# An encoder with expert-choice routing: ranking tokens in four groups of tiles, the last norm without delay, softmax two turns after the logits

## The chip, the cores and the metric

The kernel runs on 1 core of one Trainium2 chip. The metric is the device time of one execution in microseconds (us); of several runs the median is given. Engines are called PE (TensorE, matmuls), DVE (VectorE), ACT (ScalarE), POOL (GpSimd) and SP (the queue that issues most loads).

## What is computed

Two layers. Each has a mixer sub-layer (four branches, gates, an output projection) and an expert-choice mixture of experts; after each comes a layer norm. The change concerns the place where one goes over into the other:

```python
x = layer_norm(DEEPNORM_ALPHA * x + mix, ln1_g[l], ln1_b[l])        # mix: output projection of the mixer
cap = EC_FACTOR * T // N_EXPERTS                                    # 128 of 1024 tokens
aff = softmax(einsum('btd,de->bte', x, w_router))                   # 16 experts
gate, idx = lax.top_k(swapaxes(aff, 1, 2), cap)                     # each expert takes its 128 best tokens
xs = x[idx]                                                         # gather, then SwiGLU of each expert
```

The kernel doesn't sort indices. It finds for each expert the 128th largest affinity (the threshold), and then compares all affinities with it.

## The kernel before

1024 tokens are 8 tiles of 128 rows. In the output projection (`out_main`) PE works through the tiles in order, 48 matmuls of 512 columns each (L325 to L327, into the banks `pz`; three matmuls stand for one product in higher precision). As soon as half a tile is summed, DVE adds the residual and takes statistics (L1269, L1270).

What follows on a tile is the generator `post`: it ends the statistics (L420, L421 on DVE, L422 on POOL), turns the tile over (L1240 on PE, L1242 on ACT), forms the router logits on PE (`logits`, L1287), the softmax (`affinities`, L1294 to L1299: DVE, with the exponential L1297 on ACT), and the norm itself (`ln_apply`). In the norm, `spread` says how many of the two halves go over ACT (L432) and POOL (L433, L434); the others are two DVE instructions (L436, L437). Then the normed tile is stored twice, to X1 (L1234), from which the experts gather, and to XA (L1235), to which they add. These DMAs are issued by POOL; the X1 store of the last tile is issued by ACT.

After tiles 3, 5 and 7 a generator `topk_stage` starts, which ranks the affinities of a group of tiles (0 to 3, 4 and 5, 6 and 7). It turns the affinities over (L1343 on PE, a copy by ACT to `tkb`: L1346, or L1350 behind a DVE memset L1348 where there are fewer than 32 rows), takes the 64 largest of each half row by 8 rounds of MAX and MATCH_REPLACE on DVE (L1354, L1357), brings the halves together (L1330 moves rows to other partitions with a small matmul on PE, L1360 reads them), and sorts them by 7 pairs of DVE instructions (`ordered`: L1321 takes maxima, L1322 minima). Rows of several tiles are then merged two by two (L1330, `join` L1334, `ordered`), and merged with the best 128 so far, `TK`. The last group ends in the threshold (L1370). `topk` then counts and places the chosen tokens, and the first expert gathers (L1448) and begins on PE.

The order on every engine is the order in which the generators yield. At each turn of the main loop `side_all` gives every waiting `post` one step and every waiting `topk_stage` three steps. During the projection a stage puts in six idle steps (`lag`) at some places.

```python
        for _ in range(3):
            for g in list(lows):
```

Weights of the experts are loaded by SP into 45 shared slots meanwhile; ACT and DVE split them into two parts (L129, L130). The third sort buffer `tkb` is one of these slots too.

Of the kernel before, what the change touches and what calls it, by code (L numbers as in the profile page):

```python
# [22 lines left out]
NE = 16  # L23
# [129 lines left out]
def tile_encoder_trunk(ctx: ExitStack, tc: tile.TileContext, I, out, dbg=None, depth=DEPTH):  # L153
# [13 lines left out]
    def half(shape, dtype=F32, name="h"):  # L167
        return hp_.tile(shape, dtype, tag="H", name=name)
# [119 lines left out]
    sides, posts, lows = [], [], []  # L288
# [11 lines left out]
    def side_all():  # L300

        for g in list(posts):
            try:
                next(g)
            except StopIteration:
                posts.remove(g)
        for _ in range(3):
            for g in list(lows):
                try:
                    next(g)  # L310
                except StopIteration:
                    lows.remove(g)
        return [side_step(), bool(posts or lows)]
# [111 lines left out]
    def ln_apply(zs, mv, g, b, o, spread=1):  # L425

        if spread:
            nc.vector.scalar_tensor_tensor(mv[:, 2:3], mv[:, 0:1], -1.0, mv[:, 3:4], op0=OP.mult, op1=OP.mult)
        for hf in range(2):
            ns = slice(512 * hf, 512 * hf + 512)  # L430
            if spread and hf >= 2 - spread:
                nc.scalar.activation(o[:, ns], zs[hf], AF.Identity, scale=mv[:, 3:4], bias=mv[:, 2:3])  # L432
                nc.gpsimd.tensor_tensor(o[:, ns], o[:, ns], g[:, ns], op=OP.mult)  # L433
                nc.gpsimd.tensor_tensor(o[:, ns], o[:, ns], b[:, ns], op=OP.add)  # L434
            else:
                nc.vector.scalar_tensor_tensor(o[:, ns], zs[hf], mv[:, 0:1], g[:, ns], op0=OP.subtract, op1=OP.mult)  # L436
                nc.vector.scalar_tensor_tensor(o[:, ns], o[:, ns], mv[:, 3:4], b[:, ns], op0=OP.mult, op1=OP.add)  # L437

    def halves(x):
        return [x[:, 0:512], x[:, 512:1024]]  # L440
# [748 lines left out]
    def out_main(l, L, MG, xsrc, R, nxt):  # L1189

        CV, gw = L["CV"], L.pop("wr")
        bw = half([128, 8, NE], F32, name="bw")
        gs = sm.tile([128, 2, NE], F32, name="gs", bufs=1)
        gc = sm.tile([128, 2, NE], F32, name="gc", bufs=1)
        for i, w in ((1, bw), (0, gw)):
            nc.vector.tensor_tensor(w, gw, CV[:, 60 + 8 * i:68 + 8 * i][:, :, None].to_broadcast([128, 8, NE]),
                                    op=OP.mult)
            nc.vector.tensor_reduce(gs[:, i], w.rearrange("p k e -> p e k"), axis=AX.X, op=OP.add)
        del bw, w
        L.update(gw=gw, gc=gc)  # L1200

        LG = pair([128, D], "lg")
        bcast_row(LG[0], I["ln1_g"], l * D, D, nc.sync)
        bcast_row(LG[1], I["ln1_b"], l * D, D, nc.sync)
        xz = {}

        def xload(t):
            if t < 8:
                xz[t] = slot([128, D], F32, "xr")
                nc.sync.dma_start(xz[t], xsrc[128 * t:128 * t + 128, :])  # L1210

        def post(t, x, xt, st):
            ts = slice(128 * t, 128 * t + 128)
            mv = ln_mv(st, 4.0 * EPS)
            if t == 0:
                p = bank("pl")
                nc.tensor.matmul(p[:, 0:2 * NE], ones, gs.rearrange("p a e -> p (a e)"), start=True, stop=True)
                nc.vector.tensor_copy(gc, p[:, 0:2 * NE].rearrange("p (a e) -> p a e", a=2))
            if t < 7:
                yield  # L1220
            if t == 0:
                turned(x, xt, 0)
                yield
            pl = bank("pl")
            logits(L, xt, pl, 0)
            turned(x, xt, 1)
            if t < 7:
                yield
            logits(L, xt, pl, 1)
            affinities(L, t, pl, mv, R)  # L1230
            for _ in range(6 if t == 7 else 0):
                yield
            ln_apply(halves(x), mv, LG[0], LG[1], x, spread=1 + (t > 5))
            (nc.scalar if t == 7 else nc.gpsimd).dma_start(X1[l][ts, :], x)  # L1234
            nc.gpsimd.dma_start(XA[l][ts, :], x)  # L1235

        def turned(x, xt, hf):
            p = bank("pq")
            for k in range(4):
                nc.tensor.transpose(p[:, 128 * k:128 * k + 128],  # L1240
                                    x[:, 512 * hf + 128 * k:512 * hf + 128 * k + 128], ident)
            nc.scalar.copy(xt[:, 4 * hf:4 * hf + 4], p.rearrange("p (k s) -> p k s", k=4))  # L1242

        xload(0)
        xload(1)
        wo = {}
        BUDGET = {2: 26, 3: 28, 5: 31, 6: 35}
        for t in range(8):
            mh, ml = nxt
            if t + 1 < 8:  # L1250
                nxt = out_split(MG, t + 1)
            xload(t + 2)
            x = xz.pop(t)
            st = sm.tile([128, 2, 6], F32, name="st")
            xt = slot([128, 8, 128], F32, "xt")
            pz = [bank("pz"), bank("pz")]
            cut = {0: 8, 7: 4}.get(t, 0)
            turns = [(k, nf) for k in range(cut) for nf in range(2)] + \
                    [(k, nf) for nf in range(2) for k in range(cut, 8)]
            for i, (k, nf) in enumerate(turns):  # L1260
                ns = slice(512 * nf, 512 * nf + 512)
                if t == 0 and nf == 0:
                    wo[k] = W.get(names[l, "wo", k])
                mm3(pz[nf], mh[:, k], ml[:, k], wo[k][0][:, ns], wo[k][1][:, ns], k == 0, k == 7)
                if t == 7 and nf == 1:
                    W.done(names[l, "wo", k])
                    del wo[k]
                if k == 7:
                    nc.vector.scalar_tensor_tensor(x[:, ns], x[:, ns], 2.0 * ALPHA, pz[nf], op0=OP.mult, op1=OP.add)  # L1269
                    nc.vector.bn_stats(st[:, nf, :], x[:, ns])  # L1270
                if t and (k, nf) == (6, 1):
                    turned(x, xt, 0)
                if i % 2:
                    yield
            if t in BUDGET:
                W.budget = BUDGET[t]
            if t == 6:
                W.prep_max = 0
            if t == 7:
                del nxt  # L1280
            del mh, ml
            posts.append(post(t, x, xt, st))
            del x, xt

    def logits(L, xt, p, hf):
        for k in range(4 * hf, 4 * hf + 4):
            nc.tensor.matmul(p[:, 0:NE], xt[:, k, :], L["gw"][:, k, :], start=(k == 0), stop=(k == 7))  # L1287

    def affinities(L, t, p, mv, R):

        AF_, gc = R[0], L["gc"]
        rs = sm.tile([128, 4 + NE], F32, name="rs")
        ng = rs[:, 4:4 + NE]
        nc.vector.scalar_tensor_tensor(ng, gc[:, 0], mv[:, 0:1], p[:, 0:NE], op0=OP.mult, op1=OP.subtract)  # L1294
        nc.vector.scalar_tensor_tensor(ng, ng, mv[:, 3:4], gc[:, 1], op0=OP.mult, op1=OP.subtract)
        nc.vector.tensor_reduce(rs[:, 0:1], ng, axis=AX.X, op=OP.min)
        nc.scalar.activation(AF_[:, t, :], ng, AF.Exp, scale=-1.0, bias=rs[:, 0:1], accum_out=rs[:, 1:2])  # L1297
        nc.vector.reciprocal(rs[:, 2:3], rs[:, 1:2])
        nc.vector.tensor_scalar(AF_[:, t, :], AF_[:, t, :], rs[:, 2:3], None, op0=OP.mult)  # L1299
        if t in (3, 5, 7):  # L1300
            lows.append(topk_stage(R, {3: 0, 5: 4, 7: 6}[t], t))

    def topk_stage(R, t0, t):

# [4 lines left out]
        r = NE * nt  # L1309
# [17 lines left out]
        def moved(src, lo, n):  # L1327
            p = bank("pl")
            w = src.shape[1]
            nc.tensor.matmul(p[:n, 0:w], ident[:lo + n, lo:lo + n], src[:lo + n], start=True, stop=True)  # L1330
            return p[:n, 0:w]

        def join(i, u, v, n):
            nc.vector.tensor_tensor(TB[i][:n], u[:n], v[:n, ::-1], op=OP.max)  # L1334
# [4 lines left out]
        TB = [tb[:, i, :] for i in range(8)]  # L1339
# [23 lines left out]
        if t == 7:  # L1363
            while stages[0] != t0:
                yield
            join(3, TK, TB[2], NE)
            q = moved(TB[2][:r], NE, NE)
            yield from ordered(3, NE)
            join(3, TB[4], q, NE)
            nc.vector.tensor_reduce(TK[:, 0:1], TB[3][:NE], axis=AX.X, op=OP.min)  # L1370
            return
        n, i = r, 2
# [326 lines left out]
    for l in range(depth):  # L1699
# [19 lines left out]
        R = (AF_, half([NE, 128], F32, "TK"), [0])  # L1719
# [47 lines left out]
```

## Time and profile before

| | before |
|---|---|
| median of 3 runs | 3200.58 us (3200.43 to 3203.56) |
| the profiled execution | 3198.24 us |
| its span | 3196.5 us |
| granted PE clock, mean of the span | 0.981 |
| PE, DVE, ACT, POOL busy | 3046.6, 2043.6, 1430.0, 477.5 us |

The profile is of one execution. A row of a timeline has the start, the duration, engine and line, what is written from what, shapes and the number of instructions; a bracket behind it is the time that the engine stood idle before it, and what ended that. A matmul of 512 columns is shown with 0.40 us, but the next one starts 0.23 us later: they overlap. The projection and the ranking lie at 845 to 990 us (first layer) and 2424 to 2566 us (second layer).

### The profile page before, as it was taken

What the parts mean: (1) busy time and instruction counts of PE and PEld (TensorE: products, weight loads), DVE (VectorE), ACT (ScalarE), POOL (GpSimd) and SP (SyncE); (2) the same over time, 40 slices, a digit from 0 to 9 for tenths busy, and PEclk for the clock granted to TensorE, in tenths of its full rate; (3) what the DMA queues carried; (4) which work ended last, traced back from release to release, by engine and by line L of the source; (5) the groups of instructions that cost most, each with busy time, mean ns of one, the idle gap of its engine ahead of it and who ended that gap; (6) DMA issues with size and microseconds to landing.
All of it is one profiled execution on the core that took longest, in us unless ns stands there. A gap on an engine that the chain in (4) does not pass through costs nothing. (4 is left out here: it accounts for less than half of the span.)

```text
span 3196.5 us, 42301 instructions
## 1 busy us (share of the span) xinstructions
PE 3046.6 (95%) x15438; PEld 2449.4 (77%) x15438; DVE 2043.6 (64%) x3480; ACT 1430.0 (45%) x2101; POOL 477.5 (15%) x476
## 2 busy tenths in 40 slices
PE   8999999999896999999999999999999789999997
PEld 7977887778775777777789787877787567777775
DVE  3435552227768888888872365422286788888887
ACT  3122223332225777777631222233322267777773
POOL 0000001004441100001130000100064300011003
PEclk9999999999997999999999999999999899999999
DMA  5312324227556999999622123432385679999993
GB/s 163 102 33 67 112 93 135 67 92 272 222 206 250 367 368 377 377 372 368 200 96 86 40 86 93 126 102 67 108 293 207 244 269 378 373 370 369 373 343 125
DMA packets 283089, 670.45 MB, mean 210 GB/s; under 512 B 26866, under 2 KB 125258, under 8 KB 282880
## 3 DMA queue, kind: packets, MB, share of 16 engines
q1 hardware_dynamic: 259616, 586.16, 49.7%
q0 software_dynamic: 22976, 80.54, 8.4%
q8 instruction: 121, 1.98, 0.2%
q10 hardware_dynamic: 288, 1.05, 0.1%
q14 instruction: 88, 0.72, 0.1%
HBM read 578.60 MB, written 89.06 MB: 209 GB/s over the span
## 5 line engine op out<-in xcount | busy, mean ns | idle before, releaser
L130 DVE TENSOR_TENSOR wlo<-wraw,whi 128x1024 fp32r<-128x1024 f32 x886 | 1080.1, 1245 | 525.5 <-ACT whi L129 519.7
L129 ACT CAST whi<-wraw 128x1024 fp32r<-128x1024 f32 x890 | 913.5, 1047 | 361.3 <-PE h L326 79.7
L325 PE MATMUL pb<-xh,whi 128*128 128x512 f32 x1344 | 549.1, 409 | 0.0
L326 PE MATMUL pb<-xl,whi 128*128 128x512 f32 x1344 | 528.8, 393 | 0.0
L327 PE MATMUL pb<-xh,wlo 128*128 128x512 f32 x1344 | 528.7, 393 | 0.0
L325 PE MATMUL h<-whi,xsT 128*128 128x512 f32 x960 | 397.9, 414 | 0.5 <-ACT xsT L1467 0.5
L326 PE MATMUL h<-wlo,xsT 128*128 128x512 f32 x960 | 380.1, 396 | 1.0 <-DVE wlo L130 1.0
L327 PE MATMUL h<-whi,xsT 128*128 128x512 f32 x960 | 379.5, 395 | 0.3 <-DVE xsT L1470 0.3
L325 PEld LDWEIGHTS pb<-xh,whi 128*128 128x128 f32 x1344 | 252.5, 188 | 78.5 <-issue 21.8
L327 PEld LDWEIGHTS pb<-xh,wlo 128*128 128x128 f32 x1344 | 252.3, 188 | 59.1
L326 PEld LDWEIGHTS pb<-xl,whi 128*128 128x128 f32 x1344 | 252.9, 188 | 52.5 <-issue 1.9
L1138 ACT ACTIVATE gt<-pb,CVh 128x512 f32<-128x512 f32 x128 | 87.7, 685 | 362.6 <-PE pb L327 341.1
L326 PEld LDWEIGHTS h<-wlo,xsT 128*128 128x128 f32 x960 | 181.6, 189 | 49.8 <-DVE hT L1470 7.2
L325 PEld LDWEIGHTS h<-whi,xsT 128*128 128x128 f32 x960 | 181.5, 189 | 46.9 <-issue 7.7
L327 PEld LDWEIGHTS h<-whi,xsT 128*128 128x128 f32 x960 | 181.0, 189 | 43.9 <-DVE xsT L1470 2.0
L325 PE MATMUL py<-whi,hT 128*128 128x512 f32 x512 | 205.3, 401 | 0.0
L326 PE MATMUL py<-wlo,hT 128*128 128x512 f32 x512 | 202.2, 395 | 3.0 <-DVE wlo L130 3.0
L327 PE MATMUL py<-whi,hT 128*128 128x512 f32 x512 | 202.3, 395 | 0.0
L325 PE MATMUL pa<-whi,xh 128*128 128x256 f32 (+1 forms) x640 | 187.3, 293 | 6.4 <-ACT whi L129 5.6
L326 PE MATMUL pa<-wlo,xh 128*128 128x256 f32 (+1 forms) x640 | 184.8, 289 | 2.3 <-DVE wlo L130 2.2
L327 PE MATMUL pa<-whi,xl 128*128 128x256 f32 (+1 forms) x640 | 183.8, 287 | 0.0
L1448 POOL DMA_INDIRECT xs<-X,idx x32 | 54.6, 1706 | 864.6 <-ACT whi L129 814.0
(384 smaller groups left out, 4445.1 us busy)
## 6 DMA issues: line engine op xcount, KB each, us to landing
wraw<-in_w_e_dram SPq DMA_DIRECT2D x768, 512.0 KB
wraw<-in_w_in_dram SPq DMA_DIRECT2D x100, 512.0 KB
GD<-gt SPq DMA_DIRECT2D x64, 512.0 KB
gl<-GD SPq DMA_DIRECT2D x64, 512.0 KB
Rb<-RD POOLq DMA_DIRECT2D x32, 256.0 KB, 4.8
wraw<-in_w_branch_dram SPq DMA_DIRECT2D x16, 512.0 KB
wraw<-YT SPq DMA_DIRECT2D x16, 512.0 KB
wraw<-in_w_out_dram SPq DMA_DIRECT2D x16, 512.0 KB
```

Of the source, the lines that this page charges most:

```text
L129: self.nc.scalar.copy(hi, raw)
L130: (self.nc.gpsimd if i in self.pool else self.nc.vector).tensor_tensor(lo, raw, hi.bitcast(F32), op=OP.subtract)
L325: nc.tensor.matmul(p, sh, mh, start=first, stop=False)
L326: nc.tensor.matmul(p, sh, ml, start=False, stop=False)
L327: nc.tensor.matmul(p, sl, mh, start=False, stop=last)
L1138: nc.scalar.activation(gt[:, 512 * hf:512 * hf + 512], p, AF.Tanh, scale=0.5, bias=CVh[:, j:j + 1])
L1448: nc.gpsimd.indirect_dma_start(out=xs, out_offset=None, in_=X1[l], in_offset=bass.IndirectOffsetOnAxis(ap=idx[:, :1], axis=0))
```

## The change

Four edits. Each turn gives the ranking four steps in place of three. The softmax of tiles 0 to 6 comes two turns after the second half of the logits. The norm of the last tile follows its softmax at once, where six turns lay between, and tile 6 uses the form with one half on DVE. The groups are now tiles 0 to 3, 4 and 5, 6, and 7; the last group is a single tile, so that its own merge falls away.

```diff
-        for _ in range(3):
+        for _ in range(4):
             for g in list(lows):
...
             logits(L, xt, pl, 1)
+            for _ in range(2 if t < 7 else 0):
+                yield
             affinities(L, t, pl, mv, R)
-            for _ in range(6 if t == 7 else 0):
-                yield
-            ln_apply(halves(x), mv, LG[0], LG[1], x, spread=1 + (t > 5))
+            ln_apply(halves(x), mv, LG[0], LG[1], x, spread=1 + (t > 6))
             (nc.scalar if t == 7 else nc.gpsimd).dma_start(X1[l][ts, :], x)
...
-        if t in (3, 5, 7):
-            lows.append(topk_stage(R, {3: 0, 5: 4, 7: 6}[t], t))
+        if t in (3, 5, 6, 7):
+            lows.append(topk_stage(R, {3: 0, 5: 4, 6: 6, 7: 7}[t], t))
...
             join(3, TK, TB[2], NE)
-            q = moved(TB[2][:r], NE, NE)
-            yield from ordered(3, NE)
-            join(3, TB[4], q, NE)
             nc.vector.tensor_reduce(TK[:, 0:1], TB[3][:NE], axis=AX.X, op=OP.min)
```

What it moves, at three places. On DVE, in the sort of the 64 rows of tiles 0 to 3 (`tkb`; `rs`, `mv` and `aff` belong to the softmax of tile 4, `xr` is its norm). Before:

```order
L1321 TENSOR_TENSOR tkb<-tkb 64x4x16
L1322 TENSOR_TENSOR tkb<-tkb 64x4x16
L1321 TENSOR_TENSOR tkb<-tkb 64x8x8
L1322 TENSOR_TENSOR tkb<-tkb 64x8x8
L1321 TENSOR_TENSOR tkb<-tkb 64x16x4
```

and now:

```order
L1322 TENSOR_TENSOR tkb<-tkb 64x4x16
L1294 SCALAR_TENSOR_TENSOR rs<-gc,mv,pl 128x16
L1295 SCALAR_TENSOR_TENSOR rs<-rs,mv,gc 128x16
L1296 TENSOR_REDUCE rs<-rs 128x1
L1298 RECIPROCAL rs<-rs 128x1
L1299 TENSOR_SCALAR aff<-aff,rs 128x16
L428 SCALAR_TENSOR_TENSOR mv<-mv 128x1
L436 SCALAR_TENSOR_TENSOR xr<-xr,mv,lg_6438 128x512
L437 SCALAR_TENSOR_TENSOR xr<-xr,mv,lg_6439 128x512
L1321 TENSOR_TENSOR tkb<-tkb 64x8x8
L1322 TENSOR_TENSOR tkb<-tkb 64x8x8
```

The softmax and the norm have moved into the middle of the sort. On PE, the matmul that takes the result of this sort (L1330 with 32 rows) stands among the big matmuls of the next tile:

```order
 L326 MATMUL pz<-wlo,mh 128x512
 L327 MATMUL pz<-whi,ml 128x512
+L1330 MATMUL pl<-tkb,cst 32x128
 L325 MATMUL pz<-whi,mh 128x512
 L326 MATMUL pz<-wlo,mh 128x512
```

It has moved forward: 18 big matmuls lie between it and the L1330 of 64 rows that opens the sort, where there were 30. On ACT, from the last tile's turning to the first weights behind it; before:

```order
L1242 COPY xt<-pq 128x512 x2
L1297 ACTIVATE aff,rs<-rs 128x16
L1346 COPY tkb<-pl 64x64
L432 ACTIVATE xr<-xr,mv 128x512 x2
L1234 DMA X_115<-xr 128x1024
L129 CAST whi<-wraw 128x1024 x3
```

and now:

```order
L1242 COPY xt<-pq 128x512 x2
L1297 ACTIVATE aff,rs<-rs 128x16
L432 ACTIVATE xr<-xr,mv 128x512 x2
L1234 DMA X_115<-xr 128x1024
L1350 COPY tkb<-pl 16x64 x2
L129 CAST whi<-wraw 128x1024 x3
```

The norm and the issue of the X1 store have moved ahead of the copies that open the last group's ranking.

## Rows read from the trace of the kernel before

**Rows 1.** The page, busy time, share of the span and instructions of PE
```profile
PE 3046.6 (95%) x15438; PEld 2449.4 (77%) x15438; DVE 2043.6 (64%) x3480; ACT 1430.0 (45%) x2101; POOL 477.5 (15%) x476
```

**Rows 2.** Timeline of PE, projection: start, duration, instruction, idle before it
```profile
844.71 0.50 PE L326 MATMUL pz<-wlo,mh 128*128 128x512 f32 x1 [2.03 <-DVE wlo L130]
...
2490.11 0.33 PE L1330 MATMUL pl<-tkb,cst 128*64 128x64 f32 x2
...
2490.71 0.39 PE L326 MATMUL pz<-wlo,mh 128*128 128x512 f32 x1
2490.94 0.39 PE L327 MATMUL pz<-whi,ml 128*128 128x512 f32 x1
...
2509.51 0.58 PE L1330 MATMUL pl<-tkb,cst 32*16 32x128 f32 x2 [2.96 <-DVE tkb L1322]
2510.02 0.80 PE L325 MATMUL pz<-whi,mh 128*128 128x512 f32 x1
...
2512.75 0.42 PE L325 MATMUL pz<-whi,mh 128*128 128x512 f32 x1
...
2529.89 0.66 PE L1240 MATMUL pq<-cst,xr 128*128 128x128 f32 x4 [0.70 <-DVE xr L1269]
```

**Rows 3.** Windows: length, busy time (count) by engine, PEclk, DMA share, GB/s
```profile
2509.50:2512.70 3.20, 3.19 (x8) 2.26 (x9) 3.17 (x19) 0.00 (x0) 1.10 (x2) 0.50 0.63 250
...
844.70:847.00 2.30, 2.29 (x10) 1.88 (x11) 2.23 (x2) 1.32 (x4) 0.00 (x0) 1.00 0.24 98
```

**Rows 4.** Timeline of DVE, second layer, from the last softmax to the threshold
```profile
2534.66 0.23 DVE L1294 SCALAR_TENSOR_TENSOR rs<-gc,mv,pl 128x16 f32<-128x16 f32 x1 [1.33 <-PE pl L1287]
...
2536.17 0.23 DVE L1299 TENSOR_SCALAR aff<-aff,rs 128x16 f32<-128x16 f32 x1
...
2537.05 0.22 DVE L1354 MAX8 tkb<-tkb 64x8 f32<-64x64 f32 x1
...
2537.92 0.21 DVE L1354 MAX8 tkb<-tkb 64x8 f32<-64x64 f32 x1
...
2544.32 0.14 DVE L428 SCALAR_TENSOR_TENSOR mv<-mv 128x1 f32<-128x1 f32 x1
...
2550.84 0.28 DVE L1334 TENSOR_TENSOR tkb<-TK,tkb 16x128 f32<-16x128 f32 x1
...
...
2554.22 0.27 DVE L1370 TENSOR_REDUCE TK<-tkb 16x1 f32<-16x128 f32 x1
```

**Rows 5.** Timeline of DVE, second layer, tiles 4 and 5: sums, sort, softmax, norm
```profile
2491.84 0.68 DVE L1269 SCALAR_TENSOR_TENSOR xr<-xr,pz 128x512 f32<-128x512 f32 x1
...
2493.17 0.20 DVE L1360 COPY tkb<-pl 64x64 f32<-64x64 f32 x1
...
2494.69 0.22 DVE L1321 TENSOR_TENSOR tkb<-tkb 64x64 f32<-64x64 f32 x1
...
2495.08 0.22 DVE L1321 TENSOR_TENSOR tkb<-tkb 64x64 f32<-64x64 f32 x1
...
2503.49 0.23 DVE L1294 SCALAR_TENSOR_TENSOR rs<-gc,mv,pl 128x16 f32<-128x16 f32 x1 [2.09 <-PE pl L1287]
...
2505.09 0.15 DVE L428 SCALAR_TENSOR_TENSOR mv<-mv 128x1 f32<-128x1 f32 x1
...
2506.60 1.28 DVE L1321 TENSOR_TENSOR tkb<-tkb 32x64 f32<-32x64 f32 x1
...
2509.29 0.67 DVE L1269 SCALAR_TENSOR_TENSOR xr<-xr,pz 128x512 f32<-128x512 f32 x1
```

**Rows 6.** Timeline of POOL, second layer, tile 5's norm
```profile
2506.22 1.59 POOL L433 TENSOR_TENSOR xr<-xr,lg 128x512 f32<-128x512 f32 x1 [5.90 <-ACT xr L432]
```

**Rows 7.** Timeline of ACT, second layer, after the last norm
```profile
2550.63 0.33 ACTq L1234 DMA_DIRECT2D X<-xr  x1
2551.00 1.99 ACT L129 CAST whi<-wraw 128x1024 fp32r<-128x1024 f32 x2 [4.93 <-POOL xr L434]
```

**Rows 8.** The page, a costly group: busy, mean ns, idle before it, releaser
```profile
L326 PE MATMUL h<-wlo,xsT 128*128 128x512 f32 x960 | 380.1, 396 | 1.0 <-DVE wlo L130 1.0
```

## The prediction

> **What bounds the kernel now.** I read the page's busy times first: TensorE (PE) works 95% of the span [rows 1], so the time is PE's work plus the places where PE stands still. Then I took PE's timeline through the output projection and the routing of each layer, because all of the change lies there, and looked for bracketed idle times; then the timelines of VectorE (DVE), ScalarE (ACT) and GpSimd (POOL) in the same stretch, to see what each gap waited for. All prices below are from the second layer; the program of the first is the same there.
>
> Two kinds of standing still are to be seen. Inside the projection PE waits at a small matmul that moves sorted rows to other partitions (L1330): 2.96 us at 2509.51, because DVE's sort is not through, and 0.70 us at 2529.89 [rows 2]. The wait of 2.96 us has a tail: in the 3.2 us behind it the granted clock is 0.50, the 1.2 GHz level, whereas behind an idle stretch of 2.03 us at 844.71 it is 1.00, 2.4 GHz [rows 2, 3]. Six matmuls from 2510.02 to 2512.75 take 2.73 us; at the usual 0.23 us, with 0.34 for the first, they would take 1.5 [rows 2]: 1.2 us lost. After the last tile there is nothing for PE until the ranking is known: from the last softmax (L1299, 2536.17) to the threshold (L1370, 2554.22) DVE needs 18.05 us [rows 4], all of it on the path.
>
> **The change, part by part.** Its switches are costed together as what the new order makes of each wait, one layer at a time.
>
> A, the first merge of tiles 0 to 3. Before, DVE sorted the 64 rows in one piece; now the softmax of tile 4, two turns later than before, and its norm stand in the middle, and PE reaches the next L1330 after 18 big matmuls in place of 30. Call the L1330 before (64x64) zero. PE: 0.60 to its second big matmul, then 17 times 0.23 [rows 2]: it stands at the next L1330 at 4.5 us. DVE: 0.1 until the projection's bank can be read, L1269 and L1270 1.33, L1360 0.20, three pairs of the sort at 0.39, that is 1.17, the softmax from L1294 to L428 1.60, then L428 to the sort's continuation 1.51, four pairs of which two are stalled, and 0.1 to PE [rows 5]. The stalled pairs are what the trace shows at the same place behind a norm: a sorting instruction takes 1.28 us instead of 0.2 while POOL works on the norm [rows 5, 6], and two pairs take 2.69 us (2506.60 to 2509.29); the other two 0.78. Sum 9.5 us. PE waits 5.0, and at half clock loses another 1.2.
>
> B, the waits of before. The L1330 that cost 2.96 and 1.2 now stands behind 24 big matmuls and is covered by them (24 x 0.23 = 5.5 us of PE, against 0.45 + 0.3 + 7 x 0.39 + 1.33 = 4.8 of DVE); the wait of 0.70 is part of D. Together they give back 4.9.
>
> C, tiles 4 and 5 turned over (L1343). PE comes to it 18 matmuls behind L1330, 0.33 + 0.34 + 17 x 0.23 = 4.6 us. DVE must first get the moved rows (0.45, most of it the matmul), join and sort 16 rows (0.3 + 7 x 0.39), do L1269 and L1270 (1.33) and tile 5's softmax (1.60, and 0.1 to PE): 6.5. PE waits 1.9, and as behind the 2.03 us of [rows 2] no clock is lost.
>
> D, the merge of tiles 4 and 5. The pattern of A again, with tile 6's norm now half on DVE: DVE takes 0.35 + 0.2 + 1.17 + 1.60 + 1.51 + 2.69 + 0.78 + 0.1 = 8.4 us from the L1330 before it, PE is there after 18 big matmuls and the two of L1343, 0.60 + 11 x 0.23 + 0.33 + 0.34 + 5 x 0.23 = 4.9 us. PE waits 3.5, and loses 1.2 to the clock.
>
> E, tile 7's softmax. Twelve sorting instructions of tiles 4 to 6 now stand on DVE ahead of the last L420, at 0.145 us (below) 1.7 us. DVE stood idle 1.33 us there [rows 4], but the reciprocal root on POOL comes after L420 and uses some of that idle time: 0.8 us remain.
>
> F, the tail. The last norm now comes at once. Its X store (L1234) is issued by ACT, and ACT's copy that starts the last group's ranking (L1350) now stands behind that issue. The issue waits for POOL's four norm instructions: L428 starts at 2544.32, ACT comes out of the issue at 2551.00 [rows 4, 7], 6.68 us later. So the first maximum of the last group starts 0.15 + 6.68 + 0.4 = 7.2 us behind L1299, where it took 0.88 (2536.17 to 2537.05). DVE is in program order, and what is left of tile 6's group is queued behind that maximum too. From there 82 instructions remain. The trace packs six of that kind into 0.87 us (2537.05 to 2537.92), 0.145 each: 11.9, and 0.8 for two trips over PE and the last pairs, that wait for each other. 12.7 us against 17.17 before (2537.05 to 2554.22); the difference is the removed merge, 3.1 us (2550.84 to 2554.22, less 0.3 for the join that stays) [rows 4], and four stalls of about 1 us that no longer hit DVE, since it stands waiting then. 7.2 + 12.7 - 18.05 = +1.9.
>
> The Trainium skill, "DMA: Bandwidth & Descriptors", section "Issuing engines are not separate DMA queues", says that starting transfers from several engines saves only the sequencer's time to start them. By that alone the store on ACT would cost nothing here; the trace has ACT standing 4.93 us before the cast behind the issue [rows 7], and by that row the ranking's copies start some 6 us late. With copies that don't wait, F would still be about +1.1 by the same rows: the copies come 4.9 us sooner, and four stalls of 1 us hit DVE again.
>
> At nothing I cost: the slot of the third sort buffer (loads of weights then wait a little; between 0 and one load, and PE waited only 1.0 us for split weights in 960 expert matmuls [rows 8]); the XA stores and the X store of tile 7, issued earlier than before, ahead of the same gather; SP's queue, whose order doesn't change; DVE's waits at L1269 that replace those at L1294, for PE's own result, with nothing urgent behind. If this cover were gone, a load would cost its transfer, 1 to 2 us.
>
> Sum: 6.2 - 4.9 + 1.9 + 4.7 + 0.8 + 1.9 = +10.6 us a layer, +21 us for two. The profiled execution took 3198.24, so 3219.3; the median of the runs shown is 2.3 above it. **I predict 3221 us.** The bounds: without the stalls by POOL A and D lose 1.9 each and D's wait comes below 2.0 us, without loss of clock: +5.6 a layer, 3211. With the clock lost in C too and E and the two trips of F uncovered, +13.5, 3228.
>
> **Rivals.** First, faster: the two turns were DVE's idle time (it waited for logits before L1294), so the sort, at four steps a turn, is through before PE asks. Then 4.9 us of waits go, and the tail loses the removed merge: -8.0 a layer, 3185. It decides at A: DVE would have to be through in 4.5 us, and the rows give 9.5. Chance 0.07.
>
> Second, no change: the expert stage is bound by its loads, and what PE loses before it is given back as weights loaded ahead. Then about 3201. Against it: PE waits for split weights 1.0 us in all [rows 8]. Chance 0.07.
>
> Third, the change slows, but POOL's norm and DVE's sort no longer meet: 3211, as above. For it: small shifts move who meets whom. Against it: the norm's own instructions (L428, L436, L437) stand ahead of the sort as at 2505.09. Chance 0.13. My forecast, with stalls: 0.73.
>
> **The numbers.** The likeliest case gives 3221; its own spread is 3214 to 3229. The third rival extends the range to 3210, and both cases on the other side stay out. About 0.2%, 6.4 us, is what a measurement of this kernel can tell from no change. Slower by more 0.85, within 0.08, faster 0.07.
>
> **What would show it.** In the changed profile PE's waits at L1330 should be near 5 us (tiles 0 to 3) and 3.5 us (tiles 4 and 5), with half clock behind each, and near 2 us at L1343; the first maximum of tile 7 some 7 us behind its softmax, released by ACT; L1299 to the threshold about 20 us, with one merge less. I am wrong if PE passes the first L1330 without waiting, if ACT's copies come before the X store, or if the experts make up the loss.

## The result, and the profile after

| | before | after |
|---|---|---|
| median | 3200.5 us (4 runs beside the change) | 3228.8 us (4 runs) |
| ratio to before | | 1.0086, 95% interval 1.0073 to 1.0098 |
| the profiled execution | 3198.24 us | 3229.88 us |
| its span, granted PE clock | 3196.5 us, 0.981 | 3227.8 us, 0.973 |

The change makes the kernel slower by 28 us; the forecast was 3221, with a spread of 3214 to 3229, so 3228.8 lies at its very edge. The time was lost where the prediction put it, but more of it in each layer: 15.3 us from the first projection matmul to the first expert matmul, not 10.6.

The page of the changed kernel, busy time, answers to [rows 1]:

```profile
PE 3060.1 (95%) x15446; PEld 2460.5 (76%) x15446; DVE 2045.9 (63%) x3564; ACT 1429.3 (44%) x2105; POOL 473.2 (15%) x472
```

PE has only eight instructions more, small ones, and yet is busy 13.5 us longer: its matmuls ran longer. DVE and POOL did about the same work. PE's timeline in the second layer's projection, which answers to [rows 2] (start, duration, instruction, idle before it and what ended it):

```profile
2511.62 0.40 PE L327 MATMUL pz<-whi,ml 128*128 128x512 f32 x1
2516.81 0.60 PE L1330 MATMUL pl<-tkb,cst 64*32 64x128 f32 x2 [4.79 <-DVE tkb L1322]
2517.34 0.79 PE L325 MATMUL pz<-whi,mh 128*128 128x512 f32 x1
...
2522.63 0.52 PE L326 MATMUL pz<-wlo,mh 128*128 128x512 f32 x1
2522.98 0.40 PE L327 MATMUL pz<-whi,ml 128*128 128x512 f32 x1
...
2534.75 0.31 PE L1343 MATMUL pl<-cst,aff 128*32 128x64 f32 x4 [1.80 <-DVE mv L428]
...
2554.52 0.58 PE L1330 MATMUL pl<-tkb,cst 32*16 32x128 f32 x2 [3.08 <-DVE tkb L1322]
...
2558.19 0.63 PE L327 MATMUL pz<-whi,ml 128*128 128x512 f32 x1
2558.61 1.72 PE L1287 MATMUL pl<-wr,xt 128*128 128x16 f32 x8
```

Three waits stand there in place of 2.96 and 0.70 us. The first layer shows the same three: 4.94, 1.82 and 3.07 us. The granted clock behind them, by windows, which answers to [rows 3] (after the busy times comes PEclk):

```profile
2516.80:2522.80 6.00, 5.99 (x17) 4.54 (x18) 2.23 (x6) 1.81 (x5) 2.28 (x4) 0.50 0.56 208
2534.70:2540.00 5.30, 5.25 (x28) 4.31 (x29) 5.09 (x14) 1.50 (x3) 3.99 (x4) 1.00 0.25 100
2554.50:2562.00 7.50, 6.80 (x25) 5.31 (x25) 5.85 (x30) 1.58 (x4) 0.34 (x1) 0.50 1.02 376
```

Behind 4.79 us the clock stays at 0.50, the 1.2 GHz level, for 6 us, behind 3.08 us to the end of the projection and beyond; behind 1.80 us it is 1.00. DVE's timeline ahead of the first wait, which answers to [rows 5]:

```profile
2509.91 0.21 DVE L1322 TENSOR_TENSOR tkb<-tkb 64x64 f32<-64x64 f32 x1
2510.04 0.21 DVE L1294 SCALAR_TENSOR_TENSOR rs<-gc,mv,pl 128x16 f32<-128x16 f32 x1
...
2511.69 0.74 DVE L436 SCALAR_TENSOR_TENSOR xr<-xr,mv,lg 128x512 f32<-128x512 f32 x1
2512.47 0.75 DVE L437 SCALAR_TENSOR_TENSOR xr<-xr,mv,lg 128x512 f32<-128x512 f32 x1
2513.14 1.28 DVE L1321 TENSOR_TENSOR tkb<-tkb 64x64 f32<-64x64 f32 x1
2514.35 0.21 DVE L1322 TENSOR_TENSOR tkb<-tkb 64x64 f32<-64x64 f32 x1
2514.59 1.17 DVE L1321 TENSOR_TENSOR tkb<-tkb 64x64 f32<-64x64 f32 x1
```

Softmax and norm stand in the middle of the sort, and behind them two sorting instructions take 1.28 and 1.17 us in place of 0.22. POOL works on the norm then, which answers to [rows 6]:

```profile
2512.75 1.59 POOL L433 TENSOR_TENSOR xr<-xr,lg 128x512 f32<-128x512 f32 x1 [8.07 <-ACT xr L432]
2514.42 1.26 POOL L434 TENSOR_TENSOR xr<-xr,lg 128x512 f32<-128x512 f32 x1
```

The tail, first DVE from the last softmax to the threshold (L1367 is L1370 of before), then ACT; they answer to [rows 4, 7]:

```profile
2565.32 0.23 DVE L1299 TENSOR_SCALAR aff<-aff,rs 128x16 f32<-128x16 f32 x1
...
2572.66 0.22 DVE L1354 MAX8 tkb<-tkb 48x8 f32<-48x64 f32 x1 [6.17 <-ACT tkb L1350]
...
2585.20 0.27 DVE L1367 TENSOR_REDUCE TK<-tkb 16x1 f32<-16x128 f32 x1
```

```profile
2571.78 0.33 ACTq L1234 DMA_DIRECT2D X<-xr  x1
2572.21 0.42 ACT L1350 COPY tkb<-pl 16x64 f32<-16x64 f32 x2 [4.99 <-POOL xr L434]
```

ACT's copies start behind the store's issue, which waited for POOL. DVE stood 6.17 us, and L1299 to the threshold took 19.88 us against 18.05.

### The profile page after: what moved, and what is told of

It is laid out like the page before. It is cut to its first block, busy times and chain, and to the rows that moved or that the text cites. A ratio compares the mean times of both kernels' runs of the same rounds, so it can differ in the third digit from the quotient of the medians.

```text
span 3227.8 us, 42413 instructions
## 1 busy us (share of the span) xinstructions
PE 3060.1 (95%) x15446; PEld 2460.5 (76%) x15446; DVE 2045.9 (63%) x3564; ACT 1429.3 (44%) x2105; POOL 473.2 (15%) x472
## 3 DMA queue, kind: packets, MB, share of 16 engines
q10 hardware_dynamic: 288, 1.05, 0.1%
## 5 line engine op out<-in xcount | busy, mean ns | idle before, releaser
L326 PE MATMUL pb<-xl,whi 128*128 128x512 f32 x1344 | 528.1, 393 | 0.0
L326 PE MATMUL h<-wlo,xsT 128*128 128x512 f32 x960 | 379.5, 395 | 1.0 <-DVE wlo L130 1.0
L326 PEld LDWEIGHTS pb<-xl,whi 128*128 128x128 f32 x1344 | 252.8, 188 | 52.7 <-issue 1.9
L326 PEld LDWEIGHTS h<-wlo,xsT 128*128 128x128 f32 x960 | 181.2, 189 | 49.9 <-DVE hT L1467 7.2
L326 PE MATMUL py<-wlo,hT 128*128 128x512 f32 x512 | 202.3, 395 | 3.0 <-DVE wlo L130 3.0
L326 PE MATMUL pa<-wlo,xh 128*128 128x256 f32 (+1 forms) x640 | 185.4, 290 | 2.2 <-DVE wlo L130 2.2
```

The source lines that it names most:

```text
L326: nc.tensor.matmul(p, sh, ml, start=False, stop=False)
```

## The experiments

All figures below are stretches of the profiled execution, in us, first layer and second layer: the projection (first to last matmul into `pz`; it begins at 829 and 2407 us in before) as a difference to before (124.2 both); "tile 7", from there to L1299; "tail", from L1299 to the threshold; "start", from the threshold to the first expert matmul; "all", the sum as a difference to before. Executions differ by some us already ahead of the change (the first projection begins between 825.5 and 831.7), so a stretch tells more than a span. Each ratio is to runs of before on the same chip (medians 3201.6 to 3202.9; for the change itself 3200.5). The two layers of "all" together lie 1 to 7 us above the difference of these medians in every row: 30.7 against 28.3 for the change, -6.4 against -13.1 for thirteen idle steps. So the stretches place a time, but a few us of each median stay unplaced.

| kernel | median | ratio, 95% interval | projection | tile 7 | tail | start | all |
|---|---|---|---|---|---|---|---|
| before | 3200.5 | 1 | 0, 0 | 5.3, 5.3 | 18.1, 18.1 | 11.1, 11.2 | 0, 0 |
| after | 3228.8 | 1.0086 [1.0073, 1.0098] | 10.6, 10.6 | 7.1, 7.1 | 19.9, 19.9 | 12.3, 12.2 | 15.4, 15.3 |
| after, three steps | 3209.6 | 1.0030 [1.0018, 1.0042] | 0.7, 1.9 | 5.2, 5.2 | 22.2, 22.2 | 12.4, 12.5 | 5.9, 7.2 |
| after, no turns | 3219.9 | 1.0053 [1.0039, 1.0067] | 8.5, 7.9 | 6.5, 7.3 | 17.4, 17.4 | 12.2, 12.3 | 10.1, 10.3 |
| after, late norm | 3215.4 | 1.0043 [1.0030, 1.0057] | 7.9, 7.8 | 7.0, 7.0 | 13.8, 13.8 | 15.8, 15.7 | 10.1, 9.8 |
| after, three groups | 3228.1 | 1.0089 [1.0074, 1.0105] | 11.1, 11.6 | 7.2, 5.4 | 19.2, 19.2 | 11.5, 11.2 | 14.5, 12.8 |
| before, four steps | 3206.9 | 1.0015 [1.0006, 1.0024] | 4.5, 3.9 | 6.7, 6.7 | 16.2, 16.2 | 11.3, 11.1 | 4.1, 3.3 |
| before, two turns | 3202.2 | 1.0002 [0.9993, 1.0011] | 0.0, 1.4 | 6.1, 6.2 | 18.1, 18.1 | 11.3, 11.3 | 1.0, 2.4 |
| before, four groups | 3208.0 | 1.0021 [1.0011, 1.0031] | 0.1, 1.7 | 7.5, 7.3 | 19.3, 19.3 | 12.4, 12.4 | 4.9, 6.1 |
| after, ten idle steps | 3217.4 | 1.0045 [1.0031, 1.0059] | -1.0, 2.1 | 8.4, 7.7 | 23.1, 23.1 | 12.6, 12.6 | 8.6, 10.9 |
| after, norm without POOL | 3223.6 | 1.0063 [1.0050, 1.0077] | 9.1, 9.2 | 5.7, 5.7 | 19.9, 19.9 | 12.4, 12.5 | 12.6, 12.7 |
| before, norm twelve turns late | 3201.6 | 0.9997 [0.9988, 1.0006] | 0.2, 1.2 | 5.8, 5.3 | 14.0, 14.0 | 15.6, 15.5 | 1.1, 1.6 |
| the same, nine idle steps | 3194.8 | 0.9976 [0.9966, 0.9985] | -5.1, -5.2 | 6.5, 7.3 | 14.0, 14.0 | 15.7, 15.6 | -3.5, -3.0 |
| the same, thirteen idle steps | 3189.8 | 0.9962 [0.9948, 0.9976] | -5.7, -5.7 | 5.3, 5.2 | 16.1, 16.1 | 15.8, 15.6 | -3.1, -3.3 |

### Each edit undone

Three steps again:

```diff
-        for _ in range(4):
+        for _ in range(3):
             for g in list(lows):
```

> The change with three ranking steps a turn again; turns, norm and groups as changed. Theory (the wait of 4.8 us at L1330 comes from four steps and two turns together, which put tile 4's softmax and norm between the pieces of the sort, with PE there after 18 matmuls): the next L1330 stands 30 matmuls away again, so the waits of 4.8 and 3.1 us go. The softmax still comes two turns late, so one wait of some 3.5 us at an L1330 remains, as before's 2.96 was, a tile later. Projection +3 to +4 us a layer against the kernel before instead of +10.6; the ranking's tail, which makes fewer steps beforehand, stays long; 3212 to 3218. Rival (the two turns alone make the waits): they stay, 3226 to 3230. Rival (the fourth step alone makes them): nothing is left in the projection, 3200 to 3206.

3209.6, a little under the 3212 expected; projection +0.7 and +1.9, tail 22.2. PE's waits in the projection (timeline):

```profile
2517.72 0.58 PE L1330 MATMUL pl<-tkb,cst 32*16 32x128 f32 x2 [3.87 <-DVE tkb L1354]
```

The waits of 4.8, 1.8 and 3.1 are gone and one is left, at the next merge (32 rows to 16): softmax and norm now split the sort that stands ahead of that one. The fourth step is needed for the loss in the projection, and it is also what keeps the tail from growing: with three steps, four groups leave more for the end.

No turns:

```diff
-            for _ in range(2 if t < 7 else 0):
-                yield
             affinities(L, t, pl, mv, R)
```

> The change without the two turns between the logits and the softmax; four steps, norm and groups as changed. Theory (four steps and two turns together): the softmax and norm of tile 4 come ahead of the sort; the long wait at the first L1330 falls to about 2 us and keeps its clock, one of about 2.8 us remains at the merge of tiles 4 and 5. Projection about +3.5 us a layer; the ACT issue still holds the last group back, about +3.5 at the threshold; 3207 to 3212. Rival (the fourth step alone makes the waits): 3226 to 3230. Rival (the turns alone make them): 3200 to 3204.

3219.9, 8 to 13 us above what I expected: the projection loses 8 us, not 3.5. PE's waits (lines from here on are two lower than in the change):

```profile
2510.62 0.63 PE L1328 MATMUL pl<-tkb,cst 64*32 64x128 f32 x2 [3.87 <-DVE tkb L1320]
2511.18 0.79 PE L325 MATMUL pz<-whi,mh 128*128 128x512 f32 x1
```

and DVE ahead of it:

```profile
2502.68 0.21 DVE L1320 TENSOR_TENSOR tkb<-tkb 64x64 f32<-64x64 f32 x1
2503.92 0.23 DVE L1292 SCALAR_TENSOR_TENSOR rs<-gc,mv,pl 128x16 f32<-128x16 f32 x1 [1.02 <-PE pl L1285]
...
2507.03 1.28 DVE L1319 TENSOR_TENSOR tkb<-tkb 64x64 f32<-64x64 f32 x1
```

The softmax stands between the pairs of the sort here too. So the theory that only steps and turns together make this order falls: the fourth step alone splits the sort of the 64 rows, and the turns add 0.9 us to the first wait and most of the second (0.30 us is left of it here, of 1.80). The third is still 3.15 us.

The last norm late again, with tile 6's norm in its form of before:

```diff
-            ln_apply(halves(x), mv, LG[0], LG[1], x, spread=1 + (t > 6))
+            for _ in range(6 if t == 7 else 0):
+                yield
+            ln_apply(halves(x), mv, LG[0], LG[1], x, spread=1 + (t > 5))
```

> The change with the last tile's norm six turns late and tile 6's norm in its form of before; steps, turns and groups as changed. Theory (term F: ACT's copies stand behind the X1 store's issue, which waits for POOL): the copies follow the softmax at once, the first maximum comes within 1 to 2 us of L1299 in place of 7.3, and L1299 to the threshold takes 13 to 15 us in place of 19.9; the waits of 4.8 and 1.8 us at tiles 4 and 5 stay. Some 4 to 6 us a layer less than the change, 3216 to 3222. If the gather's landing, 6.2 us against 5.1 before, also hangs on the early stores, it comes back to about 5.1. Rival (the tail is bound by the sort itself): 3226 to 3230.

3215.4, a shade under the range, and 13 us under the change. PE's waits (lines two higher than in the change) and the first maximum of tile 7 on DVE:

```profile
2515.65 0.60 PE L1332 MATMUL pl<-tkb,cst 64*32 64x128 f32 x2 [4.82 <-DVE tkb L1324]
...
2533.42 0.31 PE L1345 MATMUL pl<-cst,aff 128*32 128x64 f32 x4 [1.80 <-DVE mv L428]
...
2552.34 0.37 PE L1332 MATMUL pl<-tkb,cst 32*16 32x128 f32 x2 [0.66 <-DVE tkb L1324]
```

```profile
2561.37 0.23 DVE L1301 TENSOR_SCALAR aff<-aff,rs 128x16 f32<-128x16 f32 x1
...
2562.67 0.22 DVE L1356 MAX8 tkb<-tkb 48x8 f32<-48x64 f32 x1 [0.20 <-ACT tkb L1352]
```

The maximum follows L1299 by 1.3 us in place of 7.3, and the tail takes 13.8: term F stands. But "start" grows from 12.3 to 15.8; where that goes is shown below. The third wait fell from 3.08 to 0.66 us: most of it came with tile 6's norm, whose second half on DVE (L436, L437, 1.5 us) stands in front of the sort of tiles 4 and 5. The gather's landing did not come back.

Three groups again, with their merge:

```diff
-        if t in (3, 5, 6, 7):
-            lows.append(topk_stage(R, {3: 0, 5: 4, 6: 6, 7: 7}[t], t))
+        if t in (3, 5, 7):
+            lows.append(topk_stage(R, {3: 0, 5: 4, 7: 6}[t], t))
...
+            q = moved(TB[2][:r], NE, NE)
+            yield from ordered(3, NE)
+            join(3, TB[4], q, NE)
```

> The change with the three groups of before and their own last merge; steps, turns and norm as changed. Theory (the waits come from steps and turns): the 4.8 and 1.8 us at tiles 4 and 5 stay, the third stays at about 3 us or a little more; the tail has one merge more but fewer instructions of tile 6's group queued: 1 to 2 us a layer less or the same, 3224 to 3229. Rival (the fourth group costs the time, by its instructions on DVE and its places on PE): 3200 to 3210.

3228.1, as the theory had it: the waits are 4.80, 1.80 and 3.70 us (second layer), the tail is 0.7 us shorter though it has a merge more. The fourth group does not make the loss. Only "start" comes back, to 11.2 and 11.5.

### One edit alone

Before with `range(4)`:

```diff
-        for _ in range(3):
+        for _ in range(4):
             for g in list(lows):
```

> The kernel before with four ranking steps a turn and nothing else. The run without the two turns kept a wait of 3.87 us with half clock behind it, and lost 8 us a layer in the projection; the run with three steps lost 1 to 2. Theory (the fourth step alone already puts tile 4's softmax and norm into the sort): the same wait of 3.9 us at the merge of tiles 0 to 3 in place of 2.96, a second one of 1.5 to 3 us at the merge of tiles 4 and 5, projection +3 to +6 us a layer; the tail gets shorter by 1 to 2; 3203 to 3211. Rival (steps and turns only together, as I had it): 3197 to 3202, no wait above 3 us.

```profile
2504.79 0.63 PE L1330 MATMUL pl<-tkb,cst 64*32 64x128 f32 x2 [3.86 <-DVE tkb L1322]
...
2538.48 0.39 PE L1330 MATMUL pl<-tkb,cst 32*16 32x128 f32 x2 [1.43 <-DVE tkb L1322]
```

3206.9, as expected: the fourth step alone costs 4 us a layer in the projection and 1.4 at "tile 7", and the tail gives 1.9 back.

Before with the two turns:

```diff
             logits(L, xt, pl, 1)
+            for _ in range(2 if t < 7 else 0):
+                yield
             affinities(L, t, pl, mv, R)
```

> The kernel before with the two turns between logits and softmax and nothing else. Theory (the turns only move a wait by a tile, as in the run with three steps): one wait of 3.9 us at an L1330 in place of 2.96, projection +0.5 to +2 us a layer, tail as before; 3201 to 3206. Rival (the turns cost by themselves): a second long wait, +4 us a layer and more, over 3208.

3202.2, ratio 1.0002: one wait of 3.87 us in place of 2.96, at the same merge, which stands twelve big matmuls later (not a tile), and no measurable cost. By themselves the turns are harmless.

Before with four groups and without their merge (the edit of the change to the groups alone):

> The kernel before with the four groups, without the last group's own merge, and nothing else. Theory: projection within 0.5 us of before, the tail 1 to 3 us longer, since three steps a turn leave tile 6's group unfinished when tile 7's begins; and the 1.0 us between the threshold and the first expert, which all runs with four groups showed (issue of the gather 1.7 us in place of 1.04), is here too: 3204 to 3209. Rival (that 1 us comes from steps, turns or norm): the gather's issue takes 1.04 us, as in the run with three groups. Rival (the removed merge pays): under 3200.

3208.0. The projection is as before (in the second layer PE waited 0.8 us longer near its start, 2.03 us at L326, with half clock for 3.4 us behind it), the tail is 1.3 us longer, tile 7's softmax comes 2 us later behind the maxima of tile 6, and the 1.2 us at "start" is there with this edit alone.

The fourth edit, the norm, was not run alone; undone in the change it gave back 13 us. The other three cost 5, 0 and 6 us by themselves; how the other 17 us divide between the norm by itself and the edits together stays open.

### PE's place, POOL's part, and a faster kernel

The change with PE's merges further back:

```diff
-            for _ in range(6 if len(stages) == 1 else 0):
+            for _ in range(10 if len(stages) == 1 else 0):
```

> The change as it is, with ten idle steps in place of six ahead of each merge during the projection. No instruction is added or taken away; PE's small matmuls only stand further behind the big ones. Theory (the loss in the projection is PE reaching L1330 and L1343 before DVE is through): the waits of 4.8, 1.8 and 3.1 us all go, the clock stays at 1.00, the projection is 4 to 6 us a layer shorter than before, in place of 10.6 longer; the tail is longer, since less is ranked by then; 3200 to 3208. Rival (DVE's extra work or the clock by itself sets the projection's time): it stays within 2 us of the change, 3224 to 3230.

3217.4: 11 us less than the change, though 9 above my range. The three waits are gone, as the theory says. But the idle steps hold back the whole stage, its DVE work too: the first merge's L1330 now stands 24 big matmuls behind the one before it, in place of 18, and the sort of the 64 rows stands in one piece behind softmax and norm (L437 at 2503.16, then L1360 at 2503.83). So this run doesn't tell PE's place from DVE's order. A new wait has come (PE, second layer):

```profile
2511.61 1.12 PE L1240 MATMUL pq<-cst,xr 128*128 128x128 f32 x4 [2.19 <-DVE xr L1269]
2512.66 0.63 PE L1330 MATMUL pl<-tkb,cst 64*32 64x128 f32 x2
```

DVE and POOL ahead of it, and the clock behind it:

```profile
2507.45 0.64 DVE L1321 TENSOR_TENSOR tkb<-tkb 64x64 f32<-64x64 f32 x1
2508.02 0.77 DVE L1322 TENSOR_TENSOR tkb<-tkb 64x64 f32<-64x64 f32 x1
...
2510.89 0.67 DVE L1269 SCALAR_TENSOR_TENSOR xr<-xr,pz 128x512 f32<-128x512 f32 x1
```

```profile
2507.90 2.85 POOL L1149 TENSOR_TENSOR ml<-mg,mh 128x256 fp32r<-128x256 f32 x4
```

```profile
2511.60:2521.50 9.90, 9.89 (x30) 7.73 (x31) 4.08 (x16) 0.58 (x1) 0.56 (x1) 0.50 0.62 216
```

The sort now meets another work of POOL, L1149, which splits the mixer's output: five sorting instructions take 0.64 to 0.77 us in place of 0.21, DVE comes late to L1269, and PE late to the turning of the tile. And less is ranked when tile 7 comes: the tail takes 23.1.

The change with the norms of tiles 0 to 6 wholly on DVE:

```diff
-            ln_apply(halves(x), mv, LG[0], LG[1], x, spread=1 + (t > 6))
+            ln_apply(halves(x), mv, LG[0], LG[1], x, spread=2 * (t > 6))
```

> The change with the norms of tiles 0 to 6 wholly on DVE (four instructions of some 0.75 us in place of two and POOL's two). Theory (the stalls of DVE by POOL's norm are only a part of the wait): the sorting instructions of 1.2 us at the first merge take 0.2 again, 2.0 us less, and the norm 1.5 us more, so PE waits 4.2 to 4.5 us there in place of 4.8, with half clock behind it as before; 1.8 us at L1343 unchanged; the tail unchanged; 3222 to 3229. Rival (my third one: POOL's norm meeting the sort makes the loss): PE's waits fall to 3 us and less, 3208 to 3214.

3223.6. The sorting instructions behind the norm take 0.21 again, and PE's waits are 4.14, 1.81 and 2.43 us. Without the stalls (2.0 us) and with 1.4 more of norm on DVE the first wait loses 0.65 us, and the clock behind it is 0.50 for as long. So POOL and DVE need not meet for the loss. What the meeting alone is worth (3211, said the third rival) this run doesn't tell, since the norm on DVE takes most of it back.

Before with the last norm twelve turns late:

```diff
-            for _ in range(6 if t == 7 else 0):
+            for _ in range(12 if t == 7 else 0):
                 yield
```

> The kernel before with twelve turns in place of six ahead of the last tile's norm, and nothing else. Theory (where the last norm stands in the tail is worth more than the merge that the change removes): POOL's four norm instructions and ACT's issue come behind the ranking and no longer meet the sort, so the four sorting instructions of 1.2 to 1.3 us take 0.2 again: L1299 to the threshold 13.5 to 14.5 us in place of 18.05, the projection unchanged; the stores still land before the gather, 10 us behind the threshold; 3191 to 3196. Rival (the gather waits for the late stores): the gain is given back at the gather, 3198 to 3204.

3201.6, no gain. The tail falls by 4.0 to 14.0, as expected, and "start" takes all of it back. DVE behind the threshold, and POOL:

```profile
2552.15 0.27 DVE L1370 TENSOR_REDUCE TK<-tkb 16x1 f32<-16x128 f32 x1
...
2553.54 1.36 DVE L1403 TENSOR_TENSOR GE<-aff,th 128x128 bf16<-128x128 f32 x1
...
2555.14 1.30 DVE L1415 CAST aux<-Q 128x128 bf16<-128x128 f32 x1
...
2556.47 1.36 DVE L1418 TENSOR_TENSOR aux<-Q,aux 128x128 bf16<-128x128 f32 x1
...
2558.07 0.88 DVE L1423 TENSOR_TENSOR Q<-Q,GE 128x128 f32<-128x128 f32 x1
```

```profile
2553.46 1.28 POOL L433 TENSOR_TENSOR xr<-xr,lg 128x512 f32<-128x512 f32 x1 [17.54 <-ACT xr L432]
2554.82 1.42 POOL L434 TENSOR_TENSOR xr<-xr,lg 128x512 f32<-128x512 f32 x1
```

In before these four take 0.29, 0.34, 0.52 and 0.28 us, 3.5 less together; the gather's longer issue (below) makes most of the rest. The stalls had not gone: POOL's norm now meets the counting in place of the sort. The rival was right in its number, not in its cause.

The same with nine, and with thirteen idle steps:

```diff
-            for _ in range(6 if len(stages) == 1 else 0):
+            for _ in range(13 if len(stages) == 1 else 0):
```

> The kernel before with nine idle steps in place of six ahead of each merge, and the last norm twelve turns late. Theory (PE waits in the projection because it reaches the merges too early, and the last norm disturbs the tail): no wait of over 1 us at L1330 in the projection and clock 1.00 all through it, which gives back 3 to 5 us a layer, and the tail as with the late norm alone, 4 us a layer: 3182 to 3188. Rival (as in the run with ten idle steps, the sort now meets POOL's other work, L1149, and delays DVE's L1269: a new wait of 2 us at L1240 with half clock behind it): projection within 1 us of before, 3190 to 3196.

> The same with thirteen idle steps. Theory: again no wait at L1330 in the projection, 4 to 6 us a layer; less of the ranking is done when the last tile comes, so the tail is 1 to 2 us longer than with nine: 3183 to 3190. Rival (the new wait at L1240): 3190 to 3198.

3194.8 and 3189.8: both faster than before, thirteen by 13 us in the medians (ratio 0.9962). Its profiled execution, 3196.5, was the slowest of its five, and the stretches place only 6.4 us of the gain, as much as with nine (6.5); whether thirteen beats nine stays open. With thirteen, the second layer's projection, from 2495 to the last tile, by windows:

```profile
2495.00:2528.80 33.80, 33.80 (x181) 26.81 (x180) 24.34 (x90) 7.50 (x17) 16.47 (x20) 1.00 0.78 289
```

PE is busy all the time at full clock. The 5 to 6 us a layer in the projection are what the place of the merges, on PE and DVE, was worth in the kernel before; 4.9 of them are the waits of 2.96 and 0.70 us and the 1.2 us of clock, as the prediction priced them. The late norm gives nothing more. Nine came above its range, since both ranges had counted on 4 us a layer from the late norm, which the run before shows to come back at "start". It lies in its rival's range too, but the projection is 5 us shorter and not within 1 us of before: the rival's new wait at L1240 came only behind the last projection matmul, 1.05 us at 2527.06, with half clock behind it ("tile 7" takes 6.5 and 7.3). Thirteen has no such wait. Its range had the same 4 us a layer in it, so that it was met is luck to that extent.

## Why the prediction held, and where it was too small

**A, the first merge: wait right, clock too small.** 4.79 and 4.94 us, against 5.0, with the stalls as drawn. I took 1.2 us for the clock from [rows 3], where it came back after 3.2 us. Here half clock lasted 6 us: 5.64 us from 2517.34 to 2522.98 for eleven big matmuls and a turning, which take 2 x 0.34 + 9 x 0.23 + 0.35 = 3.1 at full clock, and 0.2 at L1330: 2.7 lost. As the runs without turns and with four steps alone show, the fourth step alone splits the sort; the turns, which I named with it, only deepen the wait.

**B and C: right, with two reservations.** The waits of before went, and L1343 costs 1.80 us against 1.9, with the clock at 1.00. But B's L1330 stood behind 24 big matmuls in before too; what covers it now is that softmax and norm no longer stand in the sort ahead of it. And that C's wait cost no clock was luck: in the changes with late norm and with three groups the same wait of 1.80 us was followed by 3.4 us of half clock.

**D: wait slightly over, clock too small.** 3.08 us against 3.5, and half clock to the end of the projection: 3.67 us from L1330 to the last big matmul against 0.33 + 2 x 0.34 + 3 x 0.23 + 0.35 = 2.05 at full clock, 1.6 lost. The form of tile 6's norm causes most of this wait. A to D came to 10.6 us a layer against my 6.2 - 4.9 + 1.9 + 4.7 = 7.9: summed over the second layer's projection PE's gaps grew by 6.5 (6.7 expected), and its busy time by 4.1, of which these clock losses, less the 1.2 of before, are 3.1.

**E, tile 7's softmax: 1.8 against 0.8.** I had costed DVE's queue. Most of it is again the clock: tile 7's turning and logits (L1240 1.09 us against 0.66, L1287 1.89 against 1.06) ran at half clock. In the second layer of the run with three groups they ran at full clock, and the stretch takes 5.4. In the run without POOL's norm, with four groups as here, they ran at full clock too (1.00 from 2556.3 to 2559.6), and it takes 5.7: so the queue costs about 0.4, the clock about 1.4.

**F, the tail: right.** First maximum 7.34 us behind L1299 against 7.2, released by ACT; threshold 19.88 against 19.9: +1.8 a layer. The two reasons given there for the shorter rest, 3.1 us and four stalls of about 1, come to 7.1, not to the 4.5 between 17.17 and 12.7; tile 6's instructions, queued there as the prediction says before it, make up for the difference. The Trainium skill ("DMA: Bandwidth & Descriptors", "Issuing engines are not separate DMA queues") says that issuing transfers from several engines saves only the sequencer's time to start them. That is no guide to the cost here: the wait ahead of the issue holds ACT for 4.99 us before the copies.

**Not foreseen: the start of the experts, 1.1 us a layer.** I had costed the gather at nothing. It wants 6.14 us of PE's waiting against 5.12. The issue on POOL starts 0.80 us behind the end of the instruction that computes the row numbers on DVE (L1443; L1446 of before) in place of 0.29, and lasts 1.72 us against 1.04:

```profile
2592.48 1.72 POOL L1445 DMA_INDIRECT xs<-X,idx  x1 [19.83 <-DVE ax L1449]
```

Every run with four groups has it ("start" of 12.2 and more), and of the runs with three groups only those with the norm twelve turns late, whose issue takes 1.7 to 2.0 us too; three groups with the norm at once have 11.2 and 11.5. What makes the issue longer stays open.

In sum: 2.7 for A to D, 1.0 for E, 1.1 for the start, less 0.1: 15.3 in place of 10.6. The step that failed is the price of the clock: 1.2 us, taken from one wait of 2.96 us, was used for A and D, where 2.7 and 1.6 were lost, and what stands behind the projection at half clock, 1.4 us in E, was left out. Nor does a longer wait give the price: see the first point of the last section. The result is still within the spread, at its edge; the upper bound of 3228 was made of clock lost in C, of E's queue and of F's two trips, and none of the three came: clock elsewhere and the gather took their room.

**The rivals.** The faster one fell at A, where DVE was through after 9.3 us and not 4.5. The one on loads fell: the stretches lost 30.7 us up to the first experts, and the whole profiled execution 31.6. The third fell too: the norm on POOL and the sort did meet (1.28 and 1.17 us), and even with POOL's norm taken off tiles 0 to 6 the time is 3223.6, not 3211.

## What to carry to other kernels

An order written out by turns is two orders at once: ask, for each small matmul among big ones, how many big ones stand ahead of it and how much of the other engine's work stands ahead of its input; moving the merges back by three to seven idle steps, which changes both, gained 5 us a layer in the projection, where none of the three edits that were run alone gained anything. Price a wait of PE with the clock that it leaves behind, up to the end of the half-clock stretch and beyond the stage, and give that price a range. And when a disturbing instruction is moved out of the way, look at whom it meets next: the norm on POOL cost the sort 4 us, and then the counting 3.5.

## What the runs showed of the hardware that was not expected

- How long half clock lasts does not follow from the wait ahead of it. Before with the two turns waits 3.87 us at the same L1330 in both layers, up to 936.75 and 2517.75; the clock is back 3.5 us behind the first, and 6.3 us behind the second (windows, PEclk is the third number from the end):

```profile
936.80:940.20 3.40, 3.40 (x11) 2.54 (x12) 0.47 (x3) 0.40 (x1) 1.04 (x2) 0.51 0.67 265
940.30:945.00 4.70, 4.70 (x28) 4.08 (x27) 4.18 (x26) 0.28 (x2) 0.60 (x1) 1.00 0.82 291
2521.00:2524.00 3.00, 3.00 (x9) 2.32 (x8) 1.89 (x7) 0.44 (x1) 0.00 (x0) 0.50 0.64 210
```

  Behind 4.94 and 4.79 us it came back after about 6 in the change, but behind 4.95 and 4.80 after 3.3 and 4.7 in the change with three groups. In the run with ten idle steps the program waited 2.23 us in the first layer and 2.19 in the second, with half clock for 3.4 us and for 9.9 us behind them, although [rows 2, 3] show 2.03 us with none.
- A sorting instruction on DVE that met POOL's elementwise work ended when POOL's did: L1321 at 2513.14 ends at 2514.42, POOL's L433 at 2514.34; the next stalled one ends at 2515.76, L434 at 2515.68. The shorter L1149 makes it 0.64 to 0.77 us in place of 0.21, and a cast (L1415) took 1.30 in place of 0.34. It works the other way too: L433, which began at 2512.75 while DVE's L437 was at work (0.75 us, as always), took 1.59 us against 1.26 for the L434 behind it. The Trainium skill ("GPSIMD Engine Reference", "1. Specifications") says that GpSimd shares its interfaces to SBUF with VectorE, and that instructions of VectorE in a 2-port mode or with two SBUF inputs contend. The stalled sorting instructions have two inputs, so the trace agrees; L437 has two as well, and there POOL, which began later, was the one to lose time. Which mode the cast ran in no run here shows.
- The same indirect gather was issued in 1.04 us in some kernels and in 1.7 to 2.0 us in others, though its line was never changed. Why stays open.
